# Last mixer of a three-layer network on one core: inverses of 16x16 blocks through two 8x8 blocks, elementwise work moved from GpSimd to the other engines, the queries' norm applied as a scale of the scores

## The chip, the cores and the metric

The kernel runs on one core of a Trainium2 chip. The metric is device time in microseconds (us) for one execution. Engines are named as the profile names them: PE (TensorE, matmuls), PEld (its weight loads), DVE (VectorE), ACT (ScalarE), POOL (GpSimd), SP (SyncE, which issues most DMAs).

## The reference, cut to what matters

Three layers run one after the other on 256 tokens of width 1024, all in fp32: an attention layer with an FFN, a state-space layer with a mixture of experts, and a hybrid layer. The change touches only the mixer of the hybrid layer, which joins two branches over the same projected input `z` (256 context tokens and 256 tokens of its own):

```
# branch A: differential attention, 8 heads of two 64-wide maps
q = rmsnorm_2(q, q_g); k = rmsnorm_2(k, k_g)          # per 64 channels
q = apply_axial_rope(q, ang); k = apply_axial_rope(k, ang)
s = einsum('bmhqd,bmhkd->bmhqk', q, k) * scale
p = softmax(s); pd = p[:, 0] - lam * p[:, 1]; o = pd @ v
# branch B: wkv scan, 16 heads, two directions
sa = einsum('dbhij,dbhj->dbhi', s, kk)
s = s * w - sa (x) (kk * a) + v (x) k                  # per token
y = einsum('dbhij,dbhj->dbhi', s, r)
# both branches are gated and projected, then a PEER FFN follows
```

The kernel computes branch B in chunks of 64 tokens. Within a chunk the recurrence needs the inverse of a unit lower triangular 64x64 matrix, for each of 16 heads/directions/chunks of a pair of heads.

## The kernel before, in words

The mixer is the method `layer2_mix`. It holds both branches in one software pipeline over i, with 8 pairs of heads for branch B and 8 heads for branch A. One pass runs `chain(i)`, `inverse(i+1)`, `heads(i+1)`, `scores(i+2)` and `gates(i)`:

- `rw_scores` (L1591 on) projects k, r and v of a pair of heads, computes decays for two directions d (L1614 to L1631), and builds the tiles AL, BK, MA, MR. In each direction `kk*a` (L1671) and `a*k` (L1674) are multiplied on POOL between DVE operations that write and read the same tiles (L1669, L1670, L1672, L1673, L1675). BK then feeds the matmuls of L1679 and L1686.
- `rw_inverse` (L1787 on) inverts 32 matrices of 64x64. It gathers their 16x16 diagonal blocks (128 of them, one per partition; L1800, L1801) and inverts these by forward substitution, row by row: 15 pairs of a product (L1806) and a sum (L1807) on DVE, each of which needs the row before. The result X is copied into two padded tiles, one on DVE (L1810), one transposed on POOL (L1811); transposes on PE (L1821, L1826) and products of blocks (L1840 to L1875) build the full inverse TT.
- `rw_chain` (L1709 on) walks 8 chunks, each through R (L1733 to L1738), U (L1742 to L1744), the state S (L1750 to L1758) and Y; then a group norm whose bias is added on POOL (L1780).
- `diff_head` computes one head of branch A. `diff_qk` projects k (512 columns) and q (256), squares them (L1473), sums over 64 channels by a matmul with the block matrix `bd` (L1475), and takes 1/sqrt by Sqrt on ACT and a reciprocal on DVE (`rstd`, L366 and L367). The result multiplies q or k (L1477), and the rotary embedding follows (L1480 to L1483, with L1482 on POOL). Scores, softmax and products with v stand in L1511 to L1529.

Every weight matrix passes `wpair`: SP loads a 512-column half, ACT rounds it to a high part (L445), and an engine subtracts to get the low part (L446); PE then makes three products (L421 to L423). Each matrix of `w_in2` (L1440) comes as two halves of 128x512. The engine of the subtraction is `self.weng`: DVE in the first pass (i = -2), POOL from i = EARLY = -1 on. The pools of loaded halves and of pairs hold 2 and 4.

The order of instructions on each engine is fixed when the program is built: the Tile framework plans it with its own timeline (`schedule_with_timeline_sim=True`), and inserts the semaphores. So operations of the five parts above are interleaved on every engine, and a change of one reorders the others. After the loop, `merge` projects both branches (its first branch keeps POOL for its subtractions) and `peer` follows.

Of the kernel before, what the change touches and what calls it, by code (L numbers as in the profile page):

```python
# [249 lines left out]
class K:  # L250
# [1091 lines left out]
    def layer2_mix(self):  # L1342
        nc, tc, A, mod = self.nc, self.tc, self.A, self.mod
        m2 = mod[:, 96:144]
        with ExitStack() as c:
# [11 lines left out]
            with ExitStack() as c2:  # L1357
                self.W = c2.enter_context(tc.tile_pool(name="weights2", bufs=2))
                self.load = 512
                self.Wh = c2.enter_context(tc.tile_pool(name="weights2h", bufs=4))  # L1360
                with ExitStack() as c3:
                    self.banks(c3, b=8)
                    nc.gpsimd.dma_start(h2.hi[:, :, :T], self.hc[0])  # L1363
                    nc.gpsimd.dma_start(h2.lo[:, :, :T], self.hc[1])
                    gs = self.gains
                    sq = c3.enter_context(tc.tile_pool(name="squares", bufs=1)).tile([128, KT + 3, T], F32, name="squares")
                    v = nc.vector

                    nc.scalar.activation(sq[:, KT, 0:1], self.eps, AF.Sqrt)
                    for k in range(KT):  # L1370
                        if k < 3:
                            v.tensor_mul(sq[:, k], self.x[:, k], self.x[:, k])  # L1372
                        else:
                            nc.scalar.activation(sq[:, k], self.x[:, k], AF.Square)
                    ps = [self.psum("ms") for _ in range(2)]
                    for k in range(KT):
                        a = sq[:, KT + k % 2]
                        if k < 2:
                            v.tensor_scalar(a, sq[:, k], gs[:, 0, k:k + 1], None, op0=OP.mult)
                        else:  # L1380
                            v.scalar_tensor_tensor(a, sq[:, k], gs[:, 0, k:k + 1], a, op0=OP.mult, op1=OP.add)
                        if k:
                            nc.gpsimd.tensor_add(sq[:, KT + 2], sq[:, k], sq[:, KT + 2 if k > 1 else 0])
                    for j in range(2):
                        nc.tensor.matmul(ps[0][:, :T], self.ones_d, sq[:, KT + j], start=j == 0, stop=j == 1)
                    self.scaled(self.x, self.rstd(ps[0][:, :T], eps=gs[:, 2, 0:1]), gs[:, 1], m2[:, 0:8], h2[:, :, T:])
                    nc.tensor.matmul(ps[1][:, :T], self.ones_d, sq[:, KT + 2], start=True, stop=True)
                    self.scaled(self.x, self.rstd(ps[1][:, :T]), self.pvec("final_norm"), None, self.x)
                nc.sync.dma_start(xd, self.x)
                self.banks(c2, a=2, i=1, r=2, d=2, k=1)  # L1390
                self.bank = "a"
                self.weng = nc.vector
                self.logs = True
                self.rwkv_setup(c2, h2)
                cd = ExitStack()
                self.diff_setup(cd)

                st, inv = {}, {}
                def chain(i):
                    if i >= 0:  # L1400
                        self.bank = "r"
                        self.rw_chain(i, st.pop(i), inv.pop(i), ob if i < KT - 1 else h2[:, i, T:])

                def inverse(i):
                    if 0 <= i < KT:
                        self.bank = "i"
                        inv[i] = self.rw_inverse(i, st[i][2])

                def scores(i):
                    if i < KT:  # L1410
                        self.bank = "a"
                        st[i] = self.rw_scores(i, h2)

                def heads(i):
                    if 0 <= i < KT:
                        self.bank = "d"
                        self.diff_head(i, h2, oa)

                def gates(i):
                    for t in GATES.get(i, ()):  # L1420
                        ps = self.psum("gz", "k")
                        self.wT(ps[:, :T], self.w2(50 + t), h2[:, :, T:])
                        sg = self.rt.tile([128, 2, T], F32, tag="sq", name=f"gz{t}", bufs=1)[:, 0]
                        nc.scalar.activation(sg, ps[:, :T], AF.Tanh, scale=0.5)
                        nc.sync.dma_start(sz[:, t], sg)

                for i in range(-2, KT - 1):
                    if i == EARLY:
                        self.weng = nc.gpsimd
                    chain(i); inverse(i + 1); heads(i + 1); scores(i + 2); gates(i)  # L1430

                cd.close()
                nc.sync.dma_start(self.x, xd)
                self.W = c2.enter_context(tc.tile_pool(name="weights3", bufs=WB))
                self.merge(c2, sz, oa, ob, h2, m2[:, 16:24], lambda: chain(KT - 1))
# [27 lines left out]

    def diff_qk(self, w, h, n, gain, rot, out):

        nc = self.nc
        v_ = nc.vector
        tp = self.dt
        u = self.n
        ps = self.psum("qk")  # L1470
        self.wT(ps[:, :n], w, h)
        sq = tp.tile([128, 512], F32, tag="sq", name=f"dsq{u}")
        nc.scalar.activation(sq[:, :n], ps[:, :n], AF.Square)  # L1473
        pn = self.psum("qn")
        nc.tensor.matmul(pn[:, :n], self.bd, sq[:, :n], start=True, stop=True)  # L1475
        r = self.rstd(pn[:, :n], n, scale=1.0 / 64, logs=False)
        v_.scalar_tensor_tensor(out, ps[:, :n], gain, r, op0=OP.mult, op1=OP.mult)  # L1477
        o = out[:, rot:]
        pr = self.psum("qr")
        nc.tensor.matmul(pr[:, :T], self.ropep, o, start=True, stop=True)  # L1480
        v_.tensor_mul(sq[:, :T], pr[:, :T], self.rope[:, 1])
        nc.gpsimd.tensor_mul(o, o, self.rope[:, 0])  # L1482
        v_.tensor_add(o, o, sq[:, :T])  # L1483

    def diff_head(self, hd, h2, oa):
        nc, A = self.nc, self.A
# [4 lines left out]
        k = tp.tile([128, 2 * T], F32, tag="k", name=f"dk{hd}")  # L1491
        self.diff_qk(self.w2(8 + hd), h2, 512, self.pvec("kg"), T, k)
        q = tp.tile([128, T], F32, tag="q", name=f"dq{hd}")
        self.diff_qk(self.w2(hd), hx, T, d[:, 0:1], 0, q)
        ps = self.psum("v")
        self.wT(ps, self.w2(16 + hd), h2)
        vc = tp.tile([128, 512], F32, tag="e0", name=f"dvc{hd}")
# [7 lines left out]
        for qt in range(2):  # L1505
            st = tp.tile([128, 8], F32, tag="st", name=f"dst{hd}{qt}", bufs=2)
            es = []
            for m in range(2):
                r = slice(64 * m, 64 * m + 64)
                ps = self.psum("ds")  # L1510
                nc.tensor.matmul(ps, q[r, 128 * qt:128 * qt + 128], k[r], start=True, stop=True)  # L1511
                v_.tensor_reduce(st[:, m:m + 1], ps, axis=AX.X, op=OP.max, negate=True)
                e = tp.tile([128, 512], F32, tag=f"e{m}", name=f"de{hd}{qt}{m}", bufs=1 + m)
                nc.scalar.activation(e, ps, AF.Exp, bias=st[:, m:m + 1], accum_out=st[:, 2 + m:3 + m])
                es.append(e)
            v_.reciprocal(st[:, 4:6], st[:, 2:4])
            v_.tensor_mul(st[:, 5:6], st[:, 5:6], d[:, 7:8])
# [74 lines left out]
    def rw_scores(self, i, h2):  # L1592
# [58 lines left out]
        for d in range(2):  # L1651
# [15 lines left out]
            for o in range(2):  # L1667
                rr = slice(64 * o, 64 * o + 64)
                v_.tensor_mul(ap[rr, :8, o].rearrange("p (s c) t -> p s c t", s=2), fl(kk)[rr], fl(E1)[rr])  # L1669
                v_.tensor_mul(ap[rr, 8:, o], fl(r, 0)[rr], fl(E3[:, None], 0)[rr])  # L1670
            g_.tensor_mul(t1, kk.rearrange("p s t -> p (s t)"), a)  # L1671
            v_.tensor_mul(BK5[:, :, :, 0], fl(t1), fl(E2))  # L1672
            v_.tensor_scalar(a, a, self.pvec("rw_k_a", i), self.ka1[:, i:i + 1], op0=OP.mult, op1=OP.add)  # L1673
            g_.tensor_mul(a, a, k.rearrange("p s t -> p (s t)"))  # L1674
            v_.tensor_mul(BK5[:, :, ::-1, 1] if d else BK5[:, :, :, 1], *(x.rearrange("p (s c t) -> p s c t", s=2, t=64) for x in (a, E2)))  # L1675

            ps = self.psum("mc")
# [30 lines left out]
    def rw_chain(self, i, st, TT, ob):  # L1708
# [68 lines left out]
        rs = self.rstd(ps[:, :T], eps=self.lneps[:, 0:1], scale=1.0 / 64)  # L1777
        v_.tensor_mul(yt[:, 0], yt[:, 0], rs)
        v_.tensor_scalar(yt[:, 0], yt[:, 0], self.pvec("rw_ln_g", i), self.pvec("rw_ln_b", i), op0=OP.mult, op1=OP.add)
        g_.tensor_add(yt[:, 0], yt[:, 0], bg[:, 0])  # L1780
        v_.tensor_mul(yt[:, 1], yt[:, 0], bg[:, 1])
        if isinstance(ob, Pair):
            self.split(yt[:, 1], ob)
# [3 lines left out]
    def rw_inverse(self, i, M):  # L1787
# [11 lines left out]
            for b in range(4):  # L1799
                nc.tensor.matmul(ps[32 * b:32 * b + 32, 16 * t:16 * t + 16], A[:, :, 16 * b + t], self.ident[:64, 16 * b:16 * b + 16], start=True, stop=True)  # L1800
        v_.tensor_copy(G, ps[:, :256].rearrange("p (t s) -> p t s", t=16))  # L1801
        X = p.tile([128, 16, 16], F32, tag="X", name=f"X{i}")
        nc.gpsimd.memset(X, 0.0)
        nc.gpsimd.memset(X.rearrange("p t s -> p (t s)")[:, ::17], 1.0)
        for t in range(1, 16):
            v_.tensor_mul(pr[:, :t, :t], G[:, t:t + 1, :t].to_broadcast([128, t, t]), X[:, :t, :t].rearrange("p u s -> p s u"))  # L1806
            v_.tensor_reduce(X[:, t, :t], pr[:, :t, :t], axis=AX.X, op=OP.add, negate=True)  # L1807
        for b in range(4):
            rr = slice(32 * b, 32 * b + 32)
            v_.tensor_copy(self.pad[0][rr, :, 16 * b:16 * b + 16], X[rr])  # L1810
            nc.gpsimd.tensor_copy(self.pad[1][rr, :, 16 * b:16 * b + 16], X[rr].rearrange("p t s -> p s t"))  # L1811


        dh = [slice(0, 64), slice(64, 128)]
# [393 lines left out]
```

## Time and profile before

| | |
|---|---|
| median of 3 runs | 3528.43 us (3521.77 to 3530.41) |
| the profiled execution: its time, its span | 3523.05 us, 3521.0 us |
| PE busy | 3223.7 us (92% of the span) |
| DVE busy | 2295.1 us (65%) |
| ACT busy | 1697.7 us (48%) |
| POOL busy | 711.2 us (20%) |

Busy time is counted while an instruction of the engine runs. The granted clock is the share of TensorE's full speed that the chip gave in a stretch (1.0 is 2.4 GHz, 0.5 is 1.2 GHz). The mixer's loop lies between about 1590 and 2500 us from the start of the span; times below are counted from there. A row that names a releaser says whose end finished the idle time of an engine.

### The profile page before, as it was taken

What the parts mean: (1) busy time and instruction counts of PE and PEld (TensorE: products, weight loads), DVE (VectorE), ACT (ScalarE), POOL (GpSimd) and SP (SyncE); (2) the same over time, 40 slices, a digit from 0 to 9 for tenths busy, and PEclk for the clock granted to TensorE, in tenths of its full rate; (3) what the DMA queues carried; (4) which work ended last, traced back from release to release, by engine and by line L of the source; (5) the groups of instructions that cost most, each with busy time, mean ns of one, the idle gap of its engine ahead of it and who ended that gap; (6) DMA issues with size and microseconds to landing.
All of it is one profiled execution on the core that took longest, in us unless ns stands there. A gap on an engine that the chain in (4) does not pass through costs nothing.

```text
span 3521.0 us, 67859 instructions
## 1 busy us (share of the span) xinstructions
PE 3223.7 (92%) x26784; PEld 2655.6 (75%) x26784; DVE 2295.1 (65%) x4603; ACT 1697.7 (48%) x3077; POOL 711.2 (20%) x688
## 2 busy tenths in 40 slices
PE   6989979989999999977889999989888989999999
PEld 4869967766668888745667667767778989988788
DVE  3568857853449999745656666565457777756665
ACT  4445332442236666515434444453436657755554
POOL 0000232300000000012222222222307854410000
PEclk9999987999999999988989988988789999999999
DMA  7666673468898999961111111111336545566665
GB/s 289 237 220 230 200 257 122 137 281 326 318 373 322 338 336 341 360 250 55 44 30 47 45 43 34 48 45 45 121 114 199 167 134 179 175 197 202 227 229 162
DMA packets 162436, 658.52 MB, mean 187 GB/s; under 512 B 18216, under 2 KB 37304, under 8 KB 118208
## 3 DMA queue, kind: packets, MB, share of 16 engines
q1 hardware_dynamic: 145344, 572.33, 46.3%
q0 software_dynamic: 16768, 81.80, 6.8%
q8 instruction: 212, 3.47, 0.4%
q14 instruction: 112, 0.92, 0.1%
HBM read 634.26 MB, written 19.79 MB: 186 GB/s over the span
## 4 chain that ended last, share of the span: by engine, by line
PE 41%; DVE 7%; ACT 3%; issue 2%; DMA 2%; POOL 1%; SPq 0%; ACTq 0%; POOLq 0%; DVEq 0%
PE act L423 3%; PE act L422 3%; PE act L421 3%; PE acc L422 3%; PE acc L421 3%; PE acc L423 3%; PE G L2002 2%; DVE G L1806 1%; PE mc L1686 1%; PE mc L1679 1%; ACT L363 1%; PE v L422 1%; PE qk L421 1%; PE v L421 1%; PE qk L422 1%
## 5 line engine op out<-in xcount | busy, mean ns | idle before, releaser
L428 PE MATMUL mg<-mg,xs 128*64 128x256 f32 x1408 | 183.3, 383 | 3.7 <-ACT xf L1101 3.7
L1248 ACT ACTIVATE msg<-mg 128x128 f32<-128x128 f32 (+1 forms) x154 | 42.1, 273 | 259.2 <-PE mg L428 189.8
L1363 POOL DMA_DIRECT2D h2h<-hch x1 | 1.0, 960 | 821.3 <-DVE squares L1372 821.3
L428 PEld LDWEIGHTS mg<-mg,xs 128*64 128x64 f32 x1408 | 105.1, 137 | 67.5 <-issue 16.1
L331 PE MATMUL mod<-wm,c 128*32 128x256 f32 x1152 | 97.9, 443 | 50.9 <-DMA wm<-mods 46.1
L328 POOL DMA_DIRECT2D wm<-mods x64 | 34.7, 542 | 386.6 <-PE mod L331 368.9
L331 PEld LDWEIGHTS mod<-wm,c 128*32 128x32 f32 x1152 | 37.2, 120 | 87.6 <-DMA wm<-mods 47.0
L1249 DVE TENSOR_TENSOR msg<-msg,mg 128x128 f32<-128x128 f32 (+1 forms) x154 | 43.3, 281 | 75.5 <-ACT msg L1248 74.9
L1992 POOL TENSOR_SCALAR oh<-iota,idx 128x128 f32<-128x128 f32 x44 | 58.2, 1322 | 145.7 <-PE G L2002 145.7
L367 DVE RECIPROCAL rs<-rs 128x256 f32<-128x256 f32 (+1 forms) x24 | 58.0, 2416 | 38.2 <-ACT rs L366 38.1
L2035 POOL DMA_DIRECT2D a<-ad x32 | 17.3, 542 | 285.5 <-DVE ap48l L446 127.1
L1995 ACT ACTIVATE oh<-oh,idx 128x128 f32<-128x128 f32 x212 | 69.0, 392 | 5.8 <-DVE oh L1987 5.8
L1987 DVE TENSOR_TENSOR oh<-iota,idx 128x1024 f32<-128x1024 f32 x53 | 67.7, 1280 | 0.0
L2002 PE MATMUL G<-oh 128*128 128x128 f32 x512 | 62.5, 275 | 0.0
L1152 DVE COPY mgt<-mg 128x128 f32<-128x128 f32 x44 | 12.8, 290 | 75.1 <-PE mg L1145 74.8
L2002 PEld LDWEIGHTS G<-oh 128*128 128x128 f32 x512 | 60.1, 192 | 0.0
L428 PE MATMUL ya<-md,mgt 128*64 128x512 f32 x176 | 55.1, 604 | 3.8 <-DVE mgt L1152 3.7
L1806 DVE TENSOR_TENSOR G<-G,X 128x1 f32<-128x1 f32 (+14 forms) x120 | 52.4, 437 | 3.2
L1743 ACT ACTIVATE UV<-U 64x128 f32<-64x128 f32 x64 | 17.3, 270 | 76.3 <-PE U L1742 76.1
L428 PE MATMUL yb<-md,mgt 128*64 128x512 f32 x176 | 54.0, 592 | 0.0
L1742 PE MATMUL U<-R,TT 64*64 64x64 f32 x512 | 35.5, 255 | 20.1 <-DVE R L1738 10.5
L2007 ACT COPY Gate<-G 128x288 f32<-128x288 f32 x64 | 43.3, 678 | 20.4 <-DVE acts L2006 20.4
(11879 smaller groups left out, 12847.9 us busy)
## 6 DMA issues: line engine op xcount, KB each, us to landing
mg<-m_gu SPq DMA_DIRECT2D x176, 1024.0 KB, 7.7
md<-m_dn SPq DMA_DIRECT2D x88, 1024.0 KB, 7.9
wm<-mods POOLq DMA_DIRECT2D x64, 1024.0 KB, 6.1
w<-u SPq DMA_DIRECT2D x128, 512.0 KB, 3.8
w<-v SPq DMA_DIRECT2D x128, 512.0 KB, 4.2
w<-w_in SPq DMA_DIRECT2D x132, 256.0 KB, 2.7
w<-e_gu SPq DMA_DIRECT2D x44, 512.0 KB, 4.4
w<-e_in SPq DMA_DIRECT2D x24, 512.0 KB, 4.7
```

Of the source, the lines that this page charges most:

```text
L331: nc.tensor.matmul(ps[32 * j:32 * j + 32, :256], c[:, 2 * kp + k, :], ws[:, 2 * j + k, :], start=kp + k == 0, stop=kp + k == 4)
L367: nc.vector.reciprocal(t[:, :n], t[:, :n])
L421: mm(ps, w.hi, h.hi, start=start, stop=False, **kw)
L422: mm(ps, w.hi, h.lo, start=False, stop=False, **kw)
L423: mm(ps, w.lo, h.hi, start=False, stop=stop, **kw)
L428: mm(ps, w, h, start=start, stop=stop, **kw)
L1249: v.tensor_mul(sg[:rows], sg[:rows], ps[:rows, 128:256])
L1806: v_.tensor_mul(pr[:, :t, :t], G[:, t:t + 1, :t].to_broadcast([128, t, t]), X[:, :t, :t].rearrange("p u s -> p s u"))
L1987: v_.tensor_tensor(o, iota.rearrange("p (a b i) -> p a b i", a=1, b=1).to_broadcast([128, 2, 4, 128]), idx[:, 0:2, 4 * t4:4 * t4 + 4].rear ...
L1992: nc.gpsimd.tensor_scalar(o[:, 0, t], iota, i1, w, op0=OP.is_equal, op1=OP.mult)
L1995: nc.scalar.activation(o[:, 0, t], o[:, 0, t], AF.Copy, scale=w)
L2002: nc.tensor.matmul(ps[:, 128 * t:128 * t + 128], o[:, 1, t], o[:, 0, t], start=True, stop=True)
```

## The change

In words: `self.weng` stays DVE for the whole loop. The products of L1671, L1674 and L1482 and the sum of L1780 go to DVE. The transposed padded copy of L1811 goes to ACT. The queries (rot = 0) are no longer divided by their norm ahead of the rotary embedding: their norm is found per token, as four columns, by two matmuls against two indicator columns of the two 64-wide maps (`par64`), and enters the softmax as the scale of the exponential (the row's maximum is multiplied by it on DVE, four times per head). The 16x16 inverse becomes that of its two 8x8 diagonal blocks, done at once in 7 steps, followed by the lower left block as a product of three (two products and two sums of 512 elements). The work tile of the substitution shares the slot of P2.

```
-                    if i == EARLY:
-                        self.weng = nc.gpsimd
...
-        nc.tensor.matmul(pn[:, :n], self.bd, sq[:, :n], start=True, stop=True)
-        r = self.rstd(pn[:, :n], n, scale=1.0 / 64, logs=False)
-        v_.scalar_tensor_tensor(out, ps[:, :n], gain, r, op0=OP.mult, op1=OP.mult)
+        if rot:
...            (the three lines above)
+        else:
+            for t in range(2):
+                nc.tensor.matmul(pn[:, 2 * t:2 * t + 2], sq[:, 128 * t:128 * t + 128], self.pvec("par64"), start=True, stop=True)
+            r = tp.tile([128, 4], F32, tag="qf", name=f"qf{u}")
+            nc.scalar.activation(r, pn[:, :4], AF.Sqrt, bias=self.eps, scale=1.0 / 64)
+            v_.reciprocal(r, r)
+            v_.tensor_scalar(out, ps[:, :n], gain, None, op0=OP.mult)
...
-        nc.gpsimd.tensor_mul(o, o, self.rope[:, 0])
+        v_.tensor_mul(o, o, self.rope[:, 0])
...            (diff_head)
+                f = qf[:, 2 * qt + m:2 * qt + m + 1]
+                v_.tensor_mul(st[:, 6 + m:7 + m], st[:, m:m + 1], f)
-                nc.scalar.activation(e, ps, AF.Exp, bias=st[:, m:m + 1], accum_out=st[:, 2 + m:3 + m])
+                nc.scalar.activation(e, ps, AF.Exp, bias=st[:, 6 + m:7 + m], scale=f, accum_out=st[:, 2 + m:3 + m])
...            (rw_scores, rw_chain)
-            g_.tensor_mul(t1, kk.rearrange("p s t -> p (s t)"), a)
+            v_.tensor_mul(t1, kk.rearrange("p s t -> p (s t)"), a)
-            g_.tensor_mul(a, a, k.rearrange("p s t -> p (s t)"))
+            v_.tensor_mul(a, a, k.rearrange("p s t -> p (s t)"))
-        g_.tensor_add(yt[:, 0], yt[:, 0], bg[:, 0])
+        v_.tensor_add(yt[:, 0], yt[:, 0], bg[:, 0])
...            (rw_inverse)
-        for t in range(1, 16):
-            v_.tensor_mul(pr[:, :t, :t], G[:, t:t + 1, :t].to_broadcast([128, t, t]), X[:, :t, :t].rearrange("p u s -> p s u"))
-            v_.tensor_reduce(X[:, t, :t], pr[:, :t, :t], axis=AX.X, op=OP.add, negate=True)
+        t2 = p.tile([128, 1024], F32, tag="P2", name=f"pr{i}")
+        def blocks(x):
+            return x[:, :272].rearrange("p (q r) -> p q r", q=2)[:, :, :128].rearrange("p q (t s) -> p q t s", s=16)[:, :, :, :8]
+        G8, X8 = blocks(Gp.rearrange("p a t s -> p (a t s)")), blocks(Xf)
+        for t in range(1, 8):
+            w = t2[:, :2 * t * t].rearrange("p (q s u) -> p q s u", q=2, s=t)
+            v_.tensor_mul(w, G8[:, :, t:t + 1, :t].to_broadcast([128, 2, t, t]), X8[:, :, :t, :t].rearrange("p q u s -> p q s u"))
+            v_.tensor_reduce(X8[:, :, t, :t], w, axis=AX.X, op=OP.add, negate=True)
...            (w: 8x8x8 products; W: 8x8; rows, cols: broadcast views)
+        v_.tensor_mul(w, rows(G[:, 8:, :8]), cols(X[:, :8, :8]))
+        v_.tensor_reduce(W, w, axis=AX.X, op=OP.add)
+        v_.tensor_mul(w, rows(X[:, 8:, 8:]), cols(W))
+        v_.tensor_reduce(X[:, 8:, :8], w, axis=AX.X, op=OP.add, negate=True)
-            nc.gpsimd.tensor_copy(self.pad[1][rr, :, 16 * b:16 * b + 16], X[rr].rearrange("p t s -> p s t"))
+            nc.scalar.copy(self.pad[1][rr, :, 16 * b:16 * b + 16], X[rr].rearrange("p t s -> p s t"))
```

## Rows read from the trace of the kernel before

**Rows 1.** Windows: us, then busy us of each engine, granted clock, DMA share, GB/s
```profile
1590.00:2500.00 910.00, 814.64 (x9104) 622.33 (x9103) 561.98 (x1108) 400.61 (x729) 243.91 (x222) 0.88 0.15 43
```

**Rows 2.** Chain of waits from 1590 to 2500, by line
```profile
by line: DVE G L1806 4.7%; PE mc L1686 3.2%; issue 3.2%; PE mc L1679 2.8%; ACT L363 2.5%; PE v L422 2.5%; PE qk L421 2.4%; PE v L421 2.4%; PE qk L422 2.4%; DVE X L1807 2.3%; PE v L423 2.2%; PE qk L423 2.1%; PE ga L1800 2.1%; PE ds L1511 1.9
```

**Rows 3.** Waits of PE, 1590 to 2500: us in total, times, longest
```profile
PE mc L1679 <- DVE BK L1675: 13.5, 5, 5.7
PE tb L1821 <- DVE TT L1823: 8.8, 3, 4.7
...
PE U L1742 <- DVE R L1738: 6.9, 7, 2.2
PE S L1750 <- DVE UV L1744: 5.4, 5, 1.6
PE R L1733 <- DVE S L1757: 5.1, 2, 4.0
PE tb L1821 <- DVE pad L1810: 5.0, 2, 2.9
```

**Rows 4.** Lines of DVE, 1590 to 2500, shapes together: busy us, mean ns
```profile
L1806 DVE TENSOR_TENSOR G<-G,X 128x1 f32<-128x1 f32 (+14 forms) x120 | 52.4, 437 | 3.2
...
L1807 DVE TENSOR_REDUCE X<-G 128x1 f32<-128x1 f32 (+14 forms) x120 | 28.4, 237 | 3.1
```

**Rows 5.** Lines of DVE, 1590 to 2500, each shape apart
```profile
L367 DVE RECIPROCAL rs<-rs 128x512 f32<-128x512 f32 x8 | 26.8, 3350 | 4.0 <-ACT rs L366 4.0
L1512 DVE TENSOR_REDUCE dst<-ds 128x1 f32<-128x512 f32 x32 | 21.9, 686 | 8.9 <-PE ds L1511 8.7
...
L1758 DVE TENSOR_TENSOR S<-S,WC 128x128 f32<-128x128 f32 x42 | 19.6, 466 | 0.8
...
L367 DVE RECIPROCAL rs<-rs 128x256 f32<-128x256 f32 x8 | 14.0, 1747 | 14.1 <-ACT rs L366 14.1
...
L1757 DVE TENSOR_TENSOR S<-S,S 128x128 f32<-128x128 f32 x42 | 12.1, 287 | 26.4 <-PE S L1750 26.1
...
L1481 DVE TENSOR_TENSOR dsq<-qr,rope 128x256 f32<-128x256 f32 x16 | 6.8, 422 | 3.6 <-PE qr L1480 3.1
...
L1806 DVE TENSOR_TENSOR G<-G,X 128x1 f32<-128x1 f32 x8 | 1.2, 156 | 0.2
```

**Rows 6.** Lines of POOL, 1590 to 2500
```profile
L1671 POOL TENSOR_TENSOR el<-kk,el 128x512 f32<-128x512 f32 x16 | 21.6, 1348 | 56.8 <-DVE AL L1669 30.5 <-DVE xT L1669 22.3 <-PE S L1750 2.6
L1674 POOL TENSOR_TENSOR el<-el,k 128x512 f32<-128x512 f32 x16 | 20.5, 1281 | 13.3 <-DVE el L1673 12.9 <-PE qk L423 0.4
L1811 POOL COPY pad<-X 32x256 f32<-32x256 f32 x32 | 20.5, 639 | 21.5 <-DVE X L1807 20.5
...
L446 POOL TENSOR_TENSOR w16520l<-w,w16520h 128x512 fp32r<-128x512 f32 x1 | 1.3, 1287 | 4.1 <-ACT w16520h L445 4.1
```

**Rows 7.** Line L446 over the run: min/median/max ns, first and last start
```profile
L446 DVE TENSOR_TENSOR ring1l<-w,ring1h x4: 685/693/694, 2552.1 to 2625.4; 128x512 fp32r<-128x512 f32 x4
```

**Rows 8.** Timeline, 1644.9 to 1648.6, POOL and DVE: start us, duration us
```profile
1646.18 1.25 POOL L446 TENSOR_TENSOR w16950l<-w,w16950h 128x512 fp32r<-128x512 f32 x1
...
1646.25 1.73 DVE L1672 TENSOR_TENSOR BK<-el 128x512 f32<-128x512 f32 x1 [1.44 <-POOL el L1671]
```

**Rows 9.** Timeline, DVE, two neighbouring steps of the substitution
```profile
1673.10 0.24 DVE L1806 TENSOR_TENSOR G<-G,X 128x49 f32<-128x49 f32 x1
1673.37 0.20 DVE L1807 TENSOR_REDUCE X<-G 128x7 f32<-128x49 f32 x1
```

**Rows 10.** Windows: the eight spans from L1801 to the last L1810, summed
```profile
sum 150.20, PE 126.43 PEld 92.45 DVE 135.32 ACT 55.36 POOL 52.00; mean PE 15.80 PEld 11.56 DVE 16.91 ACT 6.92 POOL 6.50
```

**Rows 11.** Lines of PE, 1590 to 2500
```profile
L1475 PE MATMUL qn<-dsq,bd 128*128 128x256 f32 x16 | 5.9, 453 | 0.0
```

**Rows 12.** Lines of ACT, 1590 to 2500
```profile
L1823 ACT COPY TT<-tb 64x256 f32<-64x256 f32 x32 | 19.2, 599 | 28.8 <-PE tb L1821 28.8
```

**Rows 13.** Waits of all engines, 1590 to 2500
```profile
DVE rs L367 <- ACT rs L366: 18.0, 8, 8.6
```

More of the change, by code (lines that the diff above doesn't have):

```diff
@@ L1474, in diff_qk @@
         pn = self.psum("qn")
-        nc.tensor.matmul(pn[:, :n], self.bd, sq[:, :n], start=True, stop=True)
-        r = self.rstd(pn[:, :n], n, scale=1.0 / 64, logs=False)
-        v_.scalar_tensor_tensor(out, ps[:, :n], gain, r, op0=OP.mult, op1=OP.mult)
+        if rot:
+            nc.tensor.matmul(pn[:, :n], self.bd, sq[:, :n], start=True, stop=True)
+            r = self.rstd(pn[:, :n], n, scale=1.0 / 64, logs=False)
+            v_.scalar_tensor_tensor(out, ps[:, :n], gain, r, op0=OP.mult, op1=OP.mult)
+        else:
[5 more added lines that the diff above has]
+            v_.tensor_scalar(out, ps[:, :n], gain, None, op0=OP.mult)
         o = out[:, rot:]
@@ L1481, in diff_qk @@
         v_.tensor_mul(sq[:, :T], pr[:, :T], self.rope[:, 1])
-        nc.gpsimd.tensor_mul(o, o, self.rope[:, 0])
+        v_.tensor_mul(o, o, self.rope[:, 0])
         v_.tensor_add(o, o, sq[:, :T])
+        return r
     def diff_head(self, hd, h2, oa):
@@ L1493, in diff_head @@
         q = tp.tile([128, T], F32, tag="q", name=f"dq{hd}")
-        self.diff_qk(self.w2(hd), hx, T, d[:, 0:1], 0, q)
+        qf = self.diff_qk(self.w2(hd), hx, T, d[:, 0:1], 0, q)
         ps = self.psum("v")
@@ L1801, in rw_inverse, with rows, cols @@
         v_.tensor_copy(G, ps[:, :256].rearrange("p (t s) -> p t s", t=16))
-        X = p.tile([128, 16, 16], F32, tag="X", name=f"X{i}")
-        nc.gpsimd.memset(X, 0.0)
-        nc.gpsimd.memset(X.rearrange("p t s -> p (t s)")[:, ::17], 1.0)
-        for t in range(1, 16):
-            v_.tensor_mul(pr[:, :t, :t], G[:, t:t + 1, :t].to_broadcast([128, t, t]), X[:, :t, :t].rearrange("p u s -> p s u"))
-            v_.tensor_reduce(X[:, t, :t], pr[:, :t, :t], axis=AX.X, op=OP.add, negate=True)
+        Xf = p.tile([128, 272], F32, tag="X", name=f"X{i}")
+        X = Xf[:, :256].rearrange("p (t s) -> p t s", t=16)
+        nc.gpsimd.memset(Xf, 0.0)
+        nc.gpsimd.memset(Xf[:, :256:17], 1.0)
+        t2 = p.tile([128, 1024], F32, tag="P2", name=f"pr{i}")
[6 more added lines that the diff above has]
+            v_.tensor_reduce(X8[:, :, t, :t], w, axis=AX.X, op=OP.add, negate=True)
+        w = t2[:, :512].rearrange("p (t s u) -> p t s u", t=8, s=8)
+        W = pr[:, :4].rearrange("p a s -> p (a s)").rearrange("p (t s) -> p t s", t=8)
+        def rows(x):
+            return x.rearrange("p t (o u) -> p t o u", o=1).to_broadcast([128, 8, 8, 8])
+        def cols(x):
+            return x.rearrange("p (o u) s -> p o s u", o=1).to_broadcast([128, 8, 8, 8])
+        v_.tensor_mul(w, rows(G[:, 8:, :8]), cols(X[:, :8, :8]))
+        v_.tensor_reduce(W, w, axis=AX.X, op=OP.add)
+        v_.tensor_mul(w, rows(X[:, 8:, 8:]), cols(W))
+        v_.tensor_reduce(X[:, 8:, :8], w, axis=AX.X, op=OP.add, negate=True)
         for b in range(4):
```

## The prediction

> **What bounds the kernel now.** I read the windows first. In the loop of the mixer, 910 us long, PE is busy for 815 us, DVE for 562, ACT for 401 and POOL for 244, and the granted clock is 0.88 [rows 1]. PE is the busiest engine, but it stands idle for 95 us, and a clock of 0.88 instead of 1.0 costs it 0.12 x 815 = 98 us more. The most that better-timed neighbours could give is therefore about 190 us; what one change gives is a part of the 95, and perhaps a part of the 98 behind it.
>
> Then the chain of waits: matmuls hold most of it, but the largest single line is the product of the substitution, L1806, with 4.7%, and its sum L1807 has 2.3% [rows 2]. Together that is 64 us of 910, so the substitution is often, not always, what the rest waits for. The waits of PE say the same from the other side: they end on DVE, at many lines with a few us each. The longest is that for BK, 13.5 us in five waits [rows 3]. No single wait is the bound; PE is nearly full and loses time in small pieces behind DVE.
>
> **The change, part by part.** The sum is made against the profiled execution (3523.05 us); the median of the runs shown is 5.4 us above it, and I add that at the end.
>
> 1. *The products between DVE operations.* On the way to BK, POOL takes 1.348 and 1.281 us for two products of 128x512 [rows 6]; DVE takes 0.69 for an operation of that shape with two SBUF inputs [rows 7]. That saves 2.63 - 1.38 = 1.25 us in each of 16 directions. In addition the DVE operation behind the first product is stretched: it took 1.73 us beside a subtraction on POOL [rows 8], about 1.0 over 0.69. So a direction is up to 2.3 us shorter. PE waited for BK five times; 5 x 2.3 = 11.5 of the 13.5 us could go [rows 3]. Other work then is late in its place, so I take 9 (bounds 0 and 13.5).
>
> 2. *The substitution.* Now it is 80.8 us for eight, 10.1 each [rows 4]. Undisturbed, a product takes 0.156 us for one element and 0.24 for 49 [rows 5, 9], which is 1.75 ns per element; a sum 0.20 for 49 [rows 9], about 0.9 ns per element over the same start. The new seven steps have 2 x (1+4+...+49) = 280 elements: products 7 x 0.156 + 0.49 = 1.6 us, sums 7 x 0.156 + 0.25 = 1.35 us. The two products of 512 elements cost 0.69 each [rows 7] and the two sums 0.686 each, by the nearest row [rows 5]: 2.75 us. In all 5.7 us, 4.4 less each, 35 us of DVE time in all. In the eight spans from the gathered blocks to the last padded copy, 150.2 us, PE is busy for 126.4 and so idle for 23.8 [rows 10]. A span of 18.8 us shrinks by 4.4, and by about 1 us more where padded copies on DVE no longer stand beside POOL: 29%. I take 29% of the idle time, 7 us (bounds 0 and 23.8). POOL's transposed copies (0.64 us [rows 6]) go to ACT, which took 0.60 for a copy of the same free size out of PSUM [rows 12]: 32 x 0.6 = 19 us on an engine that is 44% busy, while PE is still transposing the other padded tile. I cost that at nothing; without that cover it would be up to 4 x 0.6 = 2.4 us per inverse, 19 us.
>
> 3. *What POOL holds up on DVE.* L1757 and L1758 handle the same 128x128 and take 287 and 466 ns [rows 5]: L1757 has one input in PSUM, L1758 two in SBUF. The difference over 42 is 7.5 us. The fifteen old products should take 15 x 0.156 + 1240 x 0.00175 = 4.5 us by the undisturbed price, 36 for eight, but take 52.4 [rows 4]: 16 us more. I estimate 45 us of such stretching on DVE in all, these two and half as much again and more for lines with two SBUF inputs (bounds 7.5, one line, and 244, all that POOL works [rows 1]). With POOL empty it goes. The Trainium skill ("SBUF — State Buffer", section "Who interferes with whom") says that a DVE instruction with two SBUF inputs and a GpSimd instruction that reads SBUF exclude each other for the whole instruction; the pair L1757 and L1758 agrees. If this were not so and L1758 were slow by itself, this part would be worth nothing and the sum 9 us less. On the path lie PE's waits for TT, R, UV and S: 8.8 + 6.9 + 5.4 + 5.1 = 26.2 us [rows 3]. About a third of the time of the two stretched lines was stretch, so I take a third: 9 us (bounds 0 and 26).
>
> 4. *The queries' norm.* PE loses the product with bd for q (5.9 us [rows 11]) and gains two matmuls of two columns per head; I take 3 us (bounds 0 and 5.9). DVE loses a reciprocal of 1.75 us per head, 14 us [rows 5], and gains four multiplications of one element, 32 x 0.156 = 5 us [rows 5], and a reciprocal of four. No wait of PE for the queries' rows is among the long ones [rows 3], so the shorter path of q counts only by DVE's time. Sqrt keeps its place on ACT, on four columns.
>
> 5. *The clock.* Idle time goes down by 25 of 95 us by parts 1 to 3. If the 98 us lost to the clock shrank in proportion it would give 26; nothing ties it that closely, so half: 12 (bounds 0 and 33).
>
> 6. *What DVE pays.* 61 matrices, that is 122 halves, are subtracted on DVE instead of POOL (1.287 us on POOL [rows 6]): 122 x 0.69 = 84 us [rows 7]. The 32 products of part 1 add 22, the 16 rotary products and 8 additions of 128x256 add 24 x 0.42 = 10 [rows 5], the scales 6. Against these 122 us stand 35 + 14 + (45 - 16) = 78. DVE goes from 562 to about 606 us, 62% to 67%. A subtraction is shorter, but waits in DVE's queue, where POOL was free: behind a reciprocal of 3.35 us [rows 5] or an operation that waits for ACT, up to 8.6 us [rows 13]. Behind the subtraction wait the third product of its matrix (L423) and the release of the loaded half, hence SP's next load. I take 8 us (bounds 0 and 61, one us per matrix).
>
> Sum: -9 - 7 - 9 - 3 - 12 + 8 = -32 us. 3523 - 32 = 3491 for a run like the profiled one; against the median, **3496 us**. PE stays the bound. The merge and the stages behind it start earlier and keep their lengths.
>
> **The rivals.**
> - *The substitution and BK are the path.* For it: the 64 us of the chain [rows 2]. Then the 35 us of part 2 come off whole, and of part 1 16 x 2.3 = 37 us, with 12 for the clock and 3 of part 4, less 8: -79, about 3450 us. Against it: in the eight spans PE is 84% busy [rows 10], so mostly something else is done meanwhile. Chance 0.18.
> - *PE is full anyway.* The waits removed reappear at other lines, as no line has more than 13.5 us [rows 3]; only part 4 and a few us remain, and part 6 takes them: -3 - 5 + 8 = 0, 3528 us. For it: 90% busy. Against it: the idle time ends on DVE at just the lines that this shortens. Chance 0.13.
> - *The subtractions come late.* In DVE's queue each of 61 matrices delays PE by more than it did on POOL. The gains of parts 1 to 5 are 40 us; from 40 / 61 = 0.66 us per matrix on they are eaten up, and with 1 us the time is 3528 - 40 + 61 = 3549 us. For it: only two matrices are held ahead, and DVE has waits of up to 8.6 us [rows 13]. Against it: DVE stays a third idle, and the order is planned with the subtraction in it. Chance 0.13.
> - Forecast as above, own range 3478 to 3514: chance 0.56.
>
> **How the numbers follow.** A difference of 0.3% is 10.6 us, about what a measurement of this kernel can tell from no change. Faster by more: nearly all of the forecast (0.54) and the first rival (0.18), and a little of the second (0.03): 0.75. Within: 0.02 + 0.09 + 0.02 = 0.13. Slower: 0.12, the third rival but for its edge and a little of the second. The range reaches to the first rival's middle and past the second: 3450 to 3538.
>
> **What would show it.** In the changed profile POOL is nearly empty between 1590 and the end of the loop, DVE about 65 to 68% busy; L1758's line takes about 0.29 us; the substitution's lines sum to about 46 us; PE's wait for BK is under 6 us; PE is idle for 65 to 75 us in the loop and the clock is at 0.89 or more; the loop takes about 30 us less. Wrong: PE waits for low parts of weights on DVE; the loop is shorter by the substitution's whole 35 us or by nothing; L1758 stays at 0.47 with POOL empty.

## The result, and the profile after

The kernel after takes 3488.02 us (median of 4 runs, 3484.19 to 3489.14); beside it the kernel before took 3529.42 us (4 runs, 3521.77 to 3531.88). The ratio is 0.9882, 95% interval 0.9866 to 0.9898: 41 us faster, where 32 were forecast. The execution profiled of the kernel after took 3489.14 us.

Lines have moved: L1671, L1672, L1674 and L1675 are now L1681, L1682, L1684 and L1685; L1757 and L1758 are L1767 and L1768; the substitution L1806 and L1807 is L1825 and L1826 for its seven steps and L1836 to L1839 for the lower left block; the padded copies L1810 and L1811 are L1842 and L1843; BK's first matmul L1679 is L1689; the matmuls of R, U, S and the transposes tb, L1737, L1742, L1750 and L1821, are L1747, L1752, L1760 and L1853.

The first part of the page after, busy us with the share of the span and the instructions:

```profile
PE 3207.4 (92%) x26800; PEld 2648.6 (76%) x26800; DVE 2309.6 (66%) x4717; ACT 1710.9 (49%) x3107; POOL 467.2 (13%) x478
```

For the balance I cut the loop the same way in every kernel, from its first matmul with lw to the first of the merge (br). Windows of the kernel before, then of the kernel after; columns as in [rows 1]:

```profile
1566.20:2508.00 941.80, 838.09 (x9282) 641.06 (x9282) 585.44 (x1157) 417.03 (x761) 251.93 (x230) 0.87 0.16 48
```
```profile
1559.30:2467.10 907.80, 827.15 (x9239) 638.75 (x9239) 590.10 (x1258) 426.98 (x778) 9.63 (x20) 0.88 0.16 48
1583.00:2459.00 876.00, 802.69 (x9030) 619.32 (x9029) 567.56 (x1209) 412.99 (x751) 4.05 (x14) 0.89 0.14 44
```

The loop is 34.0 us shorter. The sums below are made from these rows. PE's idle time in it (length less busy time) falls from 103.7 to 80.6 us, 23 less. The time lost to the clock (one less the granted clock, times the length; with the clock to three digits, 0.873 and 0.882) falls from 119 to 107, 12 less. What is left, called PE's work at full clock here, is 719 before and 720 after. So hardly any work was taken from PE; it waits less, and what it does runs at a slightly higher clock. Between the two profiled executions another 6.9 us lie ahead of the loop, where no line was changed (see the last section), and what follows the loop, up to the end of the span, is 7.3 us longer (1020.3 against 1013.0). The second row of after answers to [rows 1]: POOL does 4 us in 876 instead of 244 in 910, and DVE is 65% busy.

Lines of DVE in the loop of the kernel before that [rows 5] does not hold, and under them those of the kernel after, 1583 to 2459, shapes apart but for L1825 and L1826; busy us, mean ns:

```profile
L1672 DVE TENSOR_TENSOR BK<-el 128x512 f32<-128x512 f32 x16 | 19.5, 1219 | 10.7 <-POOL el L1671 10.4
L1810 DVE COPY pad<-X 32x256 f32<-32x256 f32 x32 | 18.1, 564 | 0.4
L1675 DVE TENSOR_TENSOR BK<-el 128x512 f32<-128x512 f32 x16 | 15.2, 952 | 3.4 <-POOL el L1674 3.1
```
```profile
L1825 DVE TENSOR_TENSOR pr<-G,X 128x2 f32<-128x2 f32 (+6 forms) x56 | 12.6, 225 | 1.6
L1767 DVE TENSOR_TENSOR S<-S,S 128x128 f32<-128x128 f32 x40 | 11.6, 289 | 21.9 <-PE S L1760 21.5
L1768 DVE TENSOR_TENSOR S<-S,WC 128x128 f32<-128x128 f32 x40 | 11.5, 289 | 0.7
...
L1682 DVE TENSOR_TENSOR BK<-el 128x512 f32<-128x512 f32 x16 | 11.0, 686 | 0.3
...
L1826 DVE TENSOR_REDUCE X<-pr 128x2 f32<-128x2 f32 (+6 forms) x56 | 10.6, 190 | 0.9
L1842 DVE COPY pad<-X 32x256 f32<-32x256 f32 x32 | 9.0, 282 | 0.3
L1838 DVE TENSOR_TENSOR pr<-X,G 128x512 f32<-128x512 f32 x8 | 8.8, 1102 | 0.1
L1836 DVE TENSOR_TENSOR pr<-G,X 128x512 f32<-128x512 f32 x8 | 8.3, 1033 | 0.0
L1837 DVE TENSOR_REDUCE G<-pr 128x64 f32<-128x512 f32 x8 | 5.5, 683 | 0.2
L1839 DVE TENSOR_REDUCE X<-pr 128x64 f32<-128x512 f32 x8 | 5.4, 679 | 0.0
```

L1768 now takes what L1767 takes, 289 ns, where [rows 5] had 466 and 287. L1682 takes 686 ns instead of 1219, and no longer waits for POOL. The padded copy halves, 564 to 282. The six lines of the substitution sum to 51.2 us, 6.4 per inverse, where [rows 4] had 80.8.

Waits of PE in the kernel after, 1590 to 2461: us in total, times, longest.

```profile
PE S L1760 <- ACT UV L1753: 6.9, 9, 1.6
PE mc L1689 <- DVE BK L1685: 6.1, 2, 3.4
PE tb L1853 <- DVE pad L1842: 4.6, 3, 1.9
PE S L1760 <- DVE UV L1754: 4.2, 4, 1.4
PE U L1752 <- DVE R L1748: 4.2, 8, 0.9
...
PE tb L1853 <- DVE TT L1855: 3.6, 2, 3.1
```

Against [rows 3], the wait for BK falls from 13.5 to 6.1 us and that for TT from 8.8 to 3.6, and none of the 20 longest names a subtraction (L446). The longest total is now behind ACT.

### The profile page after: what moved, and what is told of

Its sections match the earlier page's. It is cut to its first block, busy times and chain, and to the rows that moved or that the text cites. A ratio compares the mean times of both kernels' runs of the same rounds, so it can differ in the third digit from the quotient of the medians.

```text
span 3487.4 us, 67773 instructions
## 1 busy us (share of the span) xinstructions
PE 3207.4 (92%) x26800; PEld 2648.6 (76%) x26800; DVE 2309.6 (66%) x4717; ACT 1710.9 (49%) x3107; POOL 467.2 (13%) x478
## 5 line engine op out<-in xcount | busy, mean ns | idle before, releaser
L1152 DVE COPY mgt<-mg 128x128 f32<-128x128 f32 x44 | 12.8, 290 | 75.0 <-PE mg L1145 74.8
L367 DVE RECIPROCAL rs<-rs 128x512 f32<-128x512 f32 (+1 forms) x16 | 44.0, 2752 | 27.7 <-ACT rs L366 27.6
L1760 PEld LDWEIGHTS S<-UV,BKt 128*64 128x64 f32 x448 | 22.3, 150 | 37.3 <-issue 13.8
L928 PE MATMUL y<-st,s5c 128*32 128x128 f32 x256 | 43.7, 320 | 6.5 <-DVE st L920 6.5
```

The source lines that it names most:

```text
L367: nc.vector.reciprocal(t[:, :n], t[:, :n])
L928: nc.tensor.matmul(py[o, 128 * j:128 * j + 128], self.s5c[:, ci + m, i0 + r], st[:, r, m, off:off + 128], start=False, stop=m == 1, skip_g ...
```

## The experiments

The change has four parts that can be built alone: the inverse (I), the subtractions on DVE (S), the other elementwise work off POOL (E) and the queries' norm (Q). My theory was the forecast's: each part takes away waits of its own, so the parts add, and S and E empty POOL and so end the stretch on DVE (the longer time that a DVE instruction takes beside work on POOL). The rival: the parts' own prices are small, and the time comes from the order that the planner makes of all five streams, which any edit changes.

**Each part alone**, on the kernel before.

I, only the block of the change in `rw_inverse` (the transposed copy stays on POOL):
```
-        for t in range(1, 16):
+        for t in range(1, 8):
...
```


> Only the 16x16 inverse through 8x8 blocks is new; everything else as before (GpSimd keeps its work, the transposed padded copy too). My theory, many small pieces behind DVE: the eight spans lose 29% less the padded copies' share, -6 us, with a share of the clock -3: about -9 us (ratio 0.9975). Theory of the substitution as the path: all the DVE time it saves (80.8 to 51.2 us measured after the change) comes off whole: -30 us or more (0.9915). Theory of the planner's luck (any edit reshuffles the order, and the times scatter by 10 to 15 us whatever the edit is): anything, unrelated to the other parts, and the four parts do not add up to -41.

S:
```
-                    if i == EARLY:
-                        self.weng = nc.gpsimd
```


> Only the weights' subtractions stay on DVE through the loop. My theory: DVE gets 84 us more work and loses the stretch from 65% of POOL's time; -6 for the stretch and the clock's share of -3, +8 for the queue: about 0 us (0.997 to 1.003). Rival, late subtractions: +15 us or more (1.004 and up), with PE's waits for low parts of weights. Rival, the lock (that POOL's occupation of DVE was the main loss): -20 us, since 159 of POOL's 244 us go here.

E (also L1674, L1482 and L1780 to DVE, and L1811 to ACT):
```
-            g_.tensor_mul(t1, kk.rearrange("p s t -> p (s t)"), a)
+            v_.tensor_mul(t1, kk.rearrange("p s t -> p (s t)"), a)
...
```


> Only the products and the sum of the scan and of the rotary embedding go from GpSimd to DVE, and the transposed padded copy to ACT; the subtractions stay on GpSimd. My theory: -9 for BK, -3 for the stretch, -2 for the padded copies, -5 for the clock: about -18 us (0.995), the largest of the four. PE's wait for BK falls under 7 us. Theory of the substitution as the path: BK's 37 us come off whole as well, -35 us (0.990). Planner's luck: any value between -15 and +15.

Q, the edits of `diff_qk` and `diff_head` (the rotary product stays on POOL):
```
+                nc.scalar.activation(e, ps, AF.Exp, bias=st[:, 6 + m:7 + m], scale=f, accum_out=st[:, 2 + m:3 + m])
...
```


> Only the queries' norm enters as a scale. My theory: -3 us of PE, -1 for 9 us less on DVE: -4 us (0.9989), not to be told from nothing. Rival: the four more small DVE operations and the exponential's own scale (777 instead of 686 ns after the change) stand on the softmax's path, +5 us. Planner's luck: as far as 15 us either way.

Measured, with the kernel before at 3529.01 us on the same chip: I 3516.63 us, ratio 0.9964 [0.9945, 0.9983], 12 us faster. S 3495.15, 0.9896 [0.9874, 0.9917], 34 faster. E 3532.67, 1.0008 [0.9991, 1.0025], no difference (4 us more). Q 3488.75, 0.9877 [0.9851, 0.9904], 40 faster, as much as the whole change. The four sum to -82 us by the medians; the whole gave -41. So the parts do not add, and three of the four are not of the size that I gave them.

Q alone is the clearest, as it does not touch what the forecast built on. Its row of L1758 (L1769 in this kernel), 1590 to 2500, and its wait of PE for BK:

```profile
L1769 DVE TENSOR_TENSOR S<-S,WC 128x128 f32<-128x128 f32 x42 | 21.0, 499 | 1.0
```
```profile
PE mc L1690 <- DVE BK L1686: 11.9, 4, 5.4
```

The stretch is all there (499 ns), PE still waits 11.9 us for BK, and its loop is yet the shortest of all (901.8 us, table below). What in Q gives the 40 us is not shown. E alone is the reverse. Its waits of PE, 1590 to 2500:

```profile
PE dt L1522 <- DVE de L1519: 12.9, 1, 12.9
...
PE mc L1679 <- DVE BK L1675: 3.9, 3, 2.4
```

The wait for BK falls to 3.9 us, as part 1 of the forecast says, but one wait of 12.9 us stands at L1522, which E does not touch, and more is lost to the clock, as its loop shows (0.84 where the kernel before had 0.87):

```profile
1569.30:2523.70 954.40, 858.72 (x9286) 660.62 (x9286) 577.64 (x1209) 431.92 (x789) 169.84 (x143) 0.84 0.16 47
```

**A change that does nothing, and an order that changes nothing else.** The first adds one fill of 128x1 per head on DVE. The second calls two of the five parts in the other order, with no instruction added or taken away.
```
+        nul = tp.tile([128, 1], F32, tag="nul", name=f"nul{hd}"); v_.memset(nul, 0.0)
```


> The kernel before with one more write of a single column on DVE per head, which nothing reads: 8 operations of about 0.15 us. It is there to let the planner order the same work anew. Theory of causes (the queries' norm and the subtractions each gain 34 to 40 us by what they take away): 3529 us, within 5. Theory of the planner's order (the work is the same to 10 us in all kernels, and the order decides 30 to 40 us of idle PE and half clock): it may land anywhere between 3485 and 3545, and a value over 12 us away from 3529 speaks for it.


```
-                    chain(i); inverse(i + 1); heads(i + 1); scores(i + 2); gates(i)
+                    chain(i); heads(i + 1); inverse(i + 1); scores(i + 2); gates(i)
```


> The kernel before with the heads traced ahead of the inverse in each pass (the priority between two independent pieces of work); no instruction is added or removed. Theory of causes: 3529 us, within 10, since no work or path changes. Theory of the planner's order: anywhere between 3485 and 3545.

With before at 3528.93 us: the first gives 3524.77, 0.9990 [0.9972, 1.0009]. Its order on PE, DVE, ACT and SP turned out to be that of the kernel before but for the eight fills, so it tells nothing of the order; it is a control of the measurement, and shows no difference. The second gives 3516.18, 0.9963 [0.9943, 0.9983]: 13 us faster from order alone, as much as the whole new inverse gave. (In the trace ACT also loads its function tables five times less, 126 instead of 131 times.) Its loop:

```profile
1564.50:2481.10 916.60, 829.62 (x9010) 637.44 (x9010) 560.41 (x1140) 402.12 (x740) 245.44 (x227) 0.87 0.16 47
```

Idle time is 87.0 us, 17 less than before, with POOL as busy as it was. But this cut flatters it: 9,010 matmuls ended in this loop and 9,282 in that of before, as more of the last pair's chain now runs beside the merge. From the same first matmul to the first of the merge's last product (res), both kernels end the same matmuls to one; before, then the order only:

```profile
1566.20:2619.20 1053.00, 933.87 (x10307) 726.15 (x10308) 625.53 (x1248) 452.76 (x829) 275.98 (x258) 0.86 0.19 56
1564.50:2606.10 1041.60, 936.40 (x10306) 732.31 (x10307) 608.93 (x1249) 444.49 (x825) 273.21 (x259) 0.86 0.19 57
```

With equal work the stretch is 11.4 us shorter instead of 25.2, and PE's idle time falls from 119.1 to 105.2 us. For comparison, E alone has no new PE instruction, and yet PE's order is another: a comparison of the two traces line by line finds 2,370 of its 26,784 matmuls in another place.

**Combinations.** Three of the four parts, or two, by the same edits.

> The changed kernel with the queries' norm put back as it was (inverse, elementwise work and subtractions as changed). If the norm's gain is its own and the parts merely do not add up because of a common floor of about 905 us for the loop, the subtractions alone still reach the floor: 3490 us, within 8. By my first theory (many small pieces) 3492. By the planner's order: anywhere between 3485 and 3545.

> The inverse and the elementwise work as changed, the subtractions on GpSimd and the queries' norm as before. With a floor reached by either of the other two parts, this one misses it: 3529 - 12 + 4 = 3520 us, within 8, by the sum of the two single runs. By my first theory 3529 - 27 = 3502. By the planner's order: anywhere between 3485 and 3545.

> Only the two parts that gained alone, on the kernel before: subtractions on DVE and the queries' norm as scale; the inverse and the elementwise work as before. Sum of the single runs: 3529 - 34 - 40 = 3455 us. Common floor: 3488, within 8. Planner's order as the cause: anywhere between 3485 and 3545. It may beat both kernels.

> The changed kernel with the elementwise work put back on GpSimd (the products before BK and in the rotary embedding, the sum, the transposed padded copy). Sum of the single runs: 3529 - 12 - 34 - 40 = 3443 us. My first theory, in which the elementwise work was worth 18 us: 3488 + 18 = 3506. Common floor: 3488, within 8.

| parts | median us | ratio [95%] | sum of the parts alone | measured |
|---|---|---|---|---|
| I, S, E | 3506.73 | 0.9923 [0.9895, 0.9950] | -42 | -22 |
| I, E | 3552.34 | 1.0053 [1.0032, 1.0074] | -8 | +23 |
| S, Q | 3511.25 | 0.9948 [0.9929, 0.9967] | -74 | -20 |
| I, S, Q | 3525.91 | 0.9986 [0.9972, 1.0000] | -86 | -5 |
| I, S, E, Q (the change) | 3488.02 | 0.9882 [0.9866, 0.9898] | -82 | -41 |

(Before stood at 3528.93 us beside the first two and at 3531.01 beside the next two.) The sums miss by 20 to 81 us. Each time has an interval of some 5 to 10 us either way, so that the smallest miss is just clear of a sum of three such intervals and the others are well clear of theirs. I and E together are slower than before, though neither is clearly so alone. E costs 4 us by itself and gains some 38 on top of the other three (3525.91 against 3488.02).

Where the loops differ, by the same cut and the same sums as above, each from one execution. The kernel with the fills has the order of before, the two with work given back to POOL (next heading) that of after, so these rows also show how far two executions of one order lie apart. The executions profiled of I, of I, S, E and of S, Q took 3530.97, 3520.47 and 3522.64 us, 11 to 14 more than their medians; their rows say less of the times above.

| kernel | loop us | PE idle | lost to the clock | PE's work at full clock |
|---|---|---|---|---|
| before | 941.8 | 103.7 | 119 | 719 |
| after | 907.8 | 80.6 | 107 | 720 |
| I | 947.9 | 100.9 | 129 | 718 |
| S | 910.1 | 82.4 | 119 | 709 |
| E | 954.4 | 95.7 | 151 | 707 |
| Q | 901.8 | 80.3 | 104 | 717 |
| fills only | 947.3 | 106.5 | 122 | 719 |
| order only | 916.6 | 87.0 | 119 | 711 |
| I, S, E | 930.1 | 91.5 | 122 | 717 |
| I, E | 958.1 | 100.8 | 150 | 708 |
| S, Q | 923.9 | 88.1 | 119 | 717 |
| I, S, Q | 932.1 | 94.8 | 127 | 710 |
| after, POOL reads | 918.1 | 93.4 | 106 | 719 |
| after, POOL writes | 916.5 | 82.2 | 114 | 721 |

The last column stays within 14 us while the loop varies by 56; in part it moves because the cut leaves a little more or less of the last chain behind it (9,010 to 9,488 matmuls lie in these loops). Most of what any of these kernels wins or loses is idle time of PE (80 to 107) and the clock (104 to 151). E and the pair I, E show that the two need not go together: their idle time is below that of before, and 30 us more go to the clock.

**The stretch by itself.** On the kernel after, POOL gets work again that nobody waits for. For every half matrix, behind a copy of one column, it makes two products of 128x256 that read SBUF (first), or four fills of the same shape that only write (second).
```
+                g.tensor_copy(self.big[:, 0:1], part.hi[:, 0, 0:1])
+                for n in range(2):
+                    g.tensor_mul(self.big, rp, rp)
```


> The changed kernel with useless work on GpSimd at the pace of the old subtractions: behind each of 122 rounded halves a copy of one column and two products of 128x256 that read SBUF and write a tile nobody reads, about 1.4 us, 176 us in all. The order of the instructions on PE, DVE, ACT and SP is that of the changed kernel, row for row, so the planner's order can't act. Theory of the stretch (POOL holds up DVE operations with two SBUF inputs, and that costs time on PE's path): DVE is 30 to 50 us busier, L1768 takes about 0.45 us again, and the time rises by 10 to 35 us (35 if it is all that the subtractions' move gained alone). Rival (the stretch lies in DVE's slack; the gain of the subtractions was the shorter subtraction or the order): DVE busier by as much, the time within 6 us of 3488.


```
+                g.tensor_copy(self.big[:, 0:1], part.hi[:, 0, 0:1])
+                for n in range(2):
+                    g.memset(self.big, float(n)); g.memset(self.big, 2.0)
```


> The same with fills in place of the products, at the same pace and with the same order on the other engines, so GpSimd writes SBUF as long but reads hardly any. If only a GpSimd instruction that reads SBUF holds up DVE operations with two SBUF inputs, L1768 stays at 0.29 us and the time within 6 us of 3488; copies and scalar operations of DVE may still be held a little. If any GpSimd work holds DVE up, the result is that of the run with products.

In both, the order on PE, DVE, ACT and SP is that of the kernel after, row for row. So between these two only POOL's work differs. Windows of the two, 1583 to 2459, and their rows of L1768 (L1777 in these kernels) and of POOL, first with reads, then with writes:

```profile
1583.00:2459.00 876.00, 792.21 (x8884) 609.61 (x8883) 592.61 (x1199) 406.19 (x737) 244.06 (x380) 0.89 0.14 43
```
```profile
L1777 DVE TENSOR_TENSOR S<-S,WC 128x128 f32<-128x128 f32 x39 | 15.3, 392 | 0.7
```
```profile
L1446 POOL TENSOR_TENSOR big<-rope 128x256 f32<-128x256 f32 x244 | 181.6, 744 | 19.3
```
```profile
1583.00:2459.00 876.00, 801.92 (x8884) 617.09 (x8885) 565.22 (x1202) 408.01 (x741) 218.37 (x624) 0.88 0.15 44
```
```profile
L1777 DVE TENSOR_TENSOR S<-S,WC 128x128 f32<-128x128 f32 x39 | 11.2, 288 | 0.7
```
```profile
L1446 POOL MEMSET big<- 128x256 f32 x488 | 153.8, 315 | 28.2
```

With reads on POOL, L1777 takes 392 ns and DVE is 592.6 us busy in the window; with writes alone 288 ns and 565.2, as without any work on POOL (289 and 567.6). So POOL's reading stretches DVE by some 25 us, and its being busy does not. That is the rule of the Trainium skill ("SBUF — State Buffer", section "Who interferes with whom"), and these rows agree with it. Part of it reaches PE: in these windows PE is idle for 83.8 us with reads, for 74.1 with writes alone and for 73.3 in the kernel after, so some 10 of the 25 us come back as waiting of PE. In the whole time they can't be told: it is 3499.79 us (0.9932 [0.9906, 0.9958]) with reads and 3497.11 (0.9908 [0.9887, 0.9929]) with writes, beside before at 3531.01. The medians are 2.7 us apart, the ratios 0.0024, and that has an interval of some 0.0033 either way, 12 us. In the two profiled loops the clock gives the waiting back (106 us lost to it with reads, 114 with writes); two executions of one order differ by up to 6 us there, so this may be chance. Both ratios lie a little above that of the kernel after (0.9882, taken beside another run of before); whether POOL's work as such costs some 9 us, or this is scatter between sets of runs, stays open.

## Why the prediction was right, point by point

The time (3496 us forecast, 3488 measured) was right, and so was the account of where the loop gains it: PE's idle time and the clock. The account of which part gives what is borne out for its mechanisms (the wait for BK, the stretch), but not for most of its prices.

- *What bounds the kernel.* Right, and the experiments make it sharper: in fourteen loops of different lengths PE's work is the same to 14 us, and mostly its idle time and the clock vary. Parts 1 to 3 were to take 25 us of idle time and the clock 12; in the profiles it is 23 and 12, or 8 for the clock by the forecast's own sum, which counts it on PE's busy time alone (106 and 98 us). PE's idle time in the loop is 73 us of 876 (65 to 75 forecast).
- *1, the products before BK (-9).* The wait shrank by 7.4 us, and in E alone by 9.6, as forecast. As a gain of its own it is not shown: E alone gains nothing.
- *2, the substitution (-7).* 6.4 us per inverse instead of the 5.7 forecast, as the two products with broadcast operands take 1033 and 1102 ns where I took 690 from a plain product of 512 elements. I alone gave -12, interval -19 to -6: the size agrees, but a reordering of the same work gave as much, so the cause of these 12 is not shown.
- *3, the stretch (-9).* The mechanism was right: it ends when POOL stops reading, and L1768's row falls to 289 ns. It also reaches PE, as forecast: in the pair of runs with the order held, 25 us of stretch gave some 10 us of PE's idle time. What that is worth in time is not settled: the pair's medians differ by 2.7 us, and anything from nothing to some 20 us fits the runs, the 9 us of the forecast among them. The 45 us of stretch were an estimate; with POOL busy for as long as in the kernel before (244 us), the pair shows 25.
- *4, the queries' norm (-3).* Alone it gave -40. The direct saving on PE cannot be more than the 5.9 us of [rows 11]; the loop's idle time fell by 23 and the clock's loss by 15. On top of the other three parts it gave some 19 (3506.73 against 3488.02). This is the term with the largest miss, and no run shows where it comes from.
- *5, the clock (-12).* 8 to 12 in the profiles of before and after, by the way of counting. (Its upper bound, 33, is not worked out in the forecast; in proportion it is 26.) That it follows the idle time by half is not a rule: S takes 21 us off the idle time with no gain at the clock, E takes 8 off and loses 32.
- *6, what DVE pays (+8).* Not seen. S alone is 34 us faster, though that holds the end of a part of the stretch and a new order as well, so the queue's own price stays unmeasured. DVE in the loop rose by 4.7 us, not by 44: what left DVE was larger than I had counted, for example 12.8 us on the two lines of BK and 9.1 on the padded copies. No subtraction stands among PE's longer waits.
- *The rivals.* "The subtractions come late" falls with S and with the waits of PE. "PE is full anyway" falls with the 23 us of idle time. "The substitution and BK are the path" would have needed -79.

So the sum of -32 came out near because its terms' misses had both signs; as far as the terms go, that is luck. What the runs show in place of the terms is this: order alone, with the same work, moves the time by 13 us; parts that are built alone or together miss their sums by up to 81 us; and with the order held, the one suspected cost that could be tried (the stretch) moves PE's idle time by some 10 us and the time by too little to tell. This fits the rival, that the planner's order decides. It is not shown for each part: for that a part would have to change with the order of everything else held, which was tried for the stretch alone. No combination that was run beats the kernel after by more than the measurement can tell (Q alone is equal to it).

## What to carry to other kernels

Where a planner orders the queues, first measure what a mere reordering does (here 13 us of 3529, 0.4%, in the one that was tried); a gain of that size that comes with an edit is not yet the edit's gain, and parts measured alone can't be added. Forecast such a kernel by its sums (the idle time and the clock's loss of the engine that bounds it) rather than by edits, since the work at full clock is what stays. To price one mechanism, hold the order: add work on an engine that nobody waits for and compare two kinds of it. To compare stretches of two profiles, cut them where the same work lies inside; a cut at a stage's first matmul can leave some of the stage before it outside.

## What was not expected of the hardware

The stage at 560 us is the state-space layer's, ahead of everything that was changed, and the instructions up to there stand in the same order in all kernels. Windows of the kernel before, of the kernel after and of the one with the order only:

```profile
560.00:600.00 40.00, 40.00 (x180) 29.41 (x178) 32.99 (x119) 1.65 (x4) 10.72 (x18) 0.52 0.03 11
```
```profile
560.00:600.00 40.00, 38.67 (x259) 29.23 (x258) 39.73 (x145) 2.46 (x6) 13.06 (x22) 0.79 0.10 35
```
```profile
560.00:600.00 40.00, 38.84 (x285) 31.32 (x287) 37.75 (x127) 7.44 (x14) 9.83 (x17) 0.87 0.19 62
```

PE is busy nearly throughout in all three, but the granted clock is 0.52, 0.79 and 0.87, and PE ends 180, 259 and 285 matmuls. So the same instructions in the same order ran at another clock in these three kernels.

It goes with the kernel and not with chance alone. PE's order is the same in all fourteen traces up to its 4,385th matmul (608 us in the kernel before). The hundred matmuls from the 4,201st on take 23.8 to 23.9 us in nine kernels, and 14.1 to 16.6 us in five: the kernel after, its two variants with work given back to POOL, the order only, and E. Those are the five in which the planner put four to eight matmuls of the same stage in another place, a little later (608 to 650 us). The nine reach the loop at 1566.2 to 1581.3 us; the kernel after and its two variants reach it at 1559.3, 1558.6 and 1560.4. So the 6.9 us that the kernel after is ahead at the loop come back in both other kernels with its order, and are more likely part of what the new order gives than scatter, though no line of that stage was changed. What sets the clock apart ahead of the first moved matmul was not tried.
